# The feed-forward of an encoder layer by Strassen's seven products of 2x2 blocks

## The chip, the cores and the metric

One core of one Trainium2 chip runs the whole program. The metric is the device time of one execution in microseconds (us), the median of several runs. Everything is 32-bit floating point. A matrix product is made of three TensorE passes over operands split in two parts, a rounded high part and the rest: high x high, high x low, low x high (`PASS` in the code).

## The reference

```python
D_MODEL = 1024; SEQ = 1024; DEC_SEQ = 512; DEPTH = 1; D_FF = 2816; NA_HEADS = 16

def rms_norm(x, g):
    y = x * lax.rsqrt(jnp.mean(x * x, axis=-1, keepdims=True) + RMS_EPS)
    return y * g

def swiglu(x, w_gate, w_up, w_down):
    return (jax.nn.silu(x @ w_gate) * (x @ w_up)) @ w_down

def run(x):                                     # DEPTH is 1: one layer
    y = neighbourhood_attention(rms_norm(x, norm_mix[0]), na_w_qkv[0], na_rpb[0], na_w_o[0])
    x = x + y
    x = x + swiglu(rms_norm(x, norm_ffn[0]), ffn_w_gate[0], ffn_w_up[0], ffn_w_down[0])
    return rms_norm(x, norm_final)

return run(x_prompt), run(x_sample)             # (1, 1024, 1024) and (1, 512, 1024)
```

The attention (8 rows x 16 columns of neighbours on a grid, with a bias table) is not touched by the change. The feed-forward is: 1536 tokens by 1024, two products with 1024 x 2816 weights, a gate, and one with 2816 x 1024.

## The kernel before

The 1536 tokens of both requests are one list of `NT` = 12 tiles of 128 tokens. First come the norm, the V projection and the bias tables, then attention by pairs of heads, with the projections of the next pair between its products. The output projection (`project`, L578) of a token tile is work that a list of chores drops in between: TensorE multiplies the attention's output `oh` by `wo`, VectorE adds the residual (L582, tile `xo`), and POOL's DMA queue stores it to `x1_d` in DRAM (L583).

The feed-forward takes the tokens in two chunks of `CH` = 768. `norm2` loads a tile from `x1_d` by ScalarE's DMA queue, `rms` squares it on ScalarE (L107), takes the power -1/2 on POOL (L111) and scales on VectorE (L114); `transpose_split` transposes it on TensorE (L121) and splits it into a high part (ScalarE, L125) and a low one (VectorE, L126). The operands `h2` of a chunk lie in SBUF, transposed, with the model dimension on the partitions.

For each of `NF` = 22 blocks of 128 columns, `gate_up` loads the gate's and the up's weights (`wblock`, SyncE's queue), splits them (`split`: a cast on ScalarE, L130, and a subtraction on VectorE, L131) and makes two halves of 384 tokens, each a group of 24 matmuls of 128x384 (L656). ScalarE's Silu and a product on VectorE (L660, L661) follow, and a split into the operand `gt` of the down projection. After every two blocks (`SL` = 2) `down` multiplies `gt` by the rows of the down weights (L674, 128x512) and adds into `acc` in SBUF (L677), which began as `x1`. `finish` makes the final norm of a tile and stores it. While the first chunk runs, the second chunk's norms are made; its transposes stand before the last `down` of the first chunk.

The order on each engine is that of the code as a scheduler arranges it from the instructions' dependencies; each engine then runs its list strictly in order. Tiles come from pools with a fixed number of buffers, so that an instruction can wait for a buffer's last reader. Pools that are closed give their room to later ones. A DMA waits in its queue's order.

## Time and profile before

| | us |
|---|---|
| median of 3 runs | 1920.95 (1920.31 to 1922.26) |
| profiled execution, span from first to last instruction | 1918.3 |
| TensorE busy in it | 1874.5 (98%) |
| VectorE busy | 957.0 (50%) |
| ScalarE busy | 689.7 (36%) |
| POOL busy | 109.0 (6%) |

The profile is of one execution. In its rows a group of instructions stands with its line, engine, operation, written tile and read tiles, shape and count; then the busy time of all, the mean duration of one in ns, and the idle time of the engine ahead of them with what ended it. Matmuls are pipelined: the busy time divided by the count is the pace, the mean is the latency. A row of the windows table has for a stretch its length, then busy time and count of TensorE, of its weight loads, of VectorE, ScalarE and POOL, then the granted TensorE clock (1.00 is full), the DMA engines' share and GB/s. A row of the timeline has start, length, engine, line and work, and in brackets the idle time before it and what ended it.

### The profile page before, as it was taken

What the parts mean: (1) busy time and instruction counts of PE and PEld (TensorE: products, weight loads), DVE (VectorE), ACT (ScalarE), POOL (GpSimd) and SP (SyncE); (2) the same over time, 40 slices, a digit from 0 to 9 for tenths busy, and PEclk for the clock granted to TensorE, in tenths of its full rate; (3) what the DMA queues carried; (4) which work ended last, traced back from release to release, by engine and by line L of the source; (5) the groups of instructions that cost most, each with busy time, mean ns of one, the idle gap of its engine ahead of it and who ended that gap; (6) DMA issues with size and microseconds to landing.
All of it is one profiled execution on the core that took longest, in us unless ns stands there. A gap on an engine that the chain in (4) does not pass through costs nothing. (4 is left out here: it accounts for less than half of the span.)

```text
span 1918.3 us, 25624 instructions
## 1 busy us (share of the span) xinstructions
PE 1874.5 (98%) x9904; PEld 1641.6 (86%) x9904; DVE 957.0 (50%) x1945; ACT 689.7 (36%) x1414; POOL 109.0 (6%) x184
## 2 busy tenths in 40 slices
PE   8999999999999999999999999999999999999998
PEld 6887777777767778899999999999899999999997
DVE  4402777777885556443344444433634433333434
ACT  4412667666875454322222222221412211121122
POOL 1110000000230001100000000000000000000001
PEclk9999999999999999999999999999999999999999
DMA  7745433333564444652222221212321112222222
GB/s 237 227 163 164 117 102 103 105 104 101 164 186 129 139 132 146 212 194 66 66 66 66 66 66 57 62 59 66 122 66 58 58 61 66 57 66 66 66 66 77
DMA packets 227578, 201.18 MB, mean 105 GB/s; under 512 B 20736, under 2 KB 201216, under 8 KB 227456
## 3 DMA queue, kind: packets, MB, share of 16 engines
q1 hardware_dynamic: 218080, 166.51, 29.5%
q0 software_dynamic: 8512, 29.89, 4.4%
q10 hardware_dynamic: 864, 3.15, 0.5%
q8 instruction: 78, 1.28, 0.3%
q14 instruction: 44, 0.36, 0.1%
HBM read 171.39 MB, written 40.65 MB: 111 GB/s over the span
## 5 line engine op out<-in xcount | busy, mean ns | idle before, releaser
L656 PE MATMUL pgf<-h2b,whl 128*128 128x384 f32 x2112 | 369.0, 334 | 0.0
L656 PE MATMUL pgf<-h,whl 128*128 128x384 f32 x2112 | 368.0, 334 | 0.0
L656 PEld LDWEIGHTS pgf<-h2b,whl 128*128 128x128 f32 x2112 | 366.4, 188 | 1.0
L656 PEld LDWEIGHTS pgf<-h,whl 128*128 128x128 f32 x2112 | 366.4, 188 | 0.8
L674 PE MATMUL pd<-wd,gt 128*128 128x512 f32 x1584 | 365.3, 390 | 0.4 <-DVE acc L677 0.4
L674 PEld LDWEIGHTS pd<-wd,gt 128*128 128x128 f32 x1584 | 296.4, 188 | 60.9 <-DVE acc L677 0.8
L677 DVE TENSOR_TENSOR acc<-acc,pd 128x512 f32<-128x512 f32 x264 | 176.9, 685 | 106.2 <-PE pd L674 106.2
L131 DVE TENSOR_TENSOR whl<-wr,whl 128x1024 fp32r<-128x1024 f32 x104 | 128.5, 1235 | 199.8 <-ACT whl L130 199.8
L660 ACT ACTIVATE sg<-pgf 128x384 f32<-128x384 f32 x88 | 43.3, 491 | 466.9 <-PE pgf L656 466.8
L661 DVE TENSOR_TENSOR sg<-sg,pgf 128x384 f32<-128x384 f32 x88 | 48.8, 554 | 296.7 <-PE pgf L656 296.7
L324 PE MATMUL pg<-hTp,whl 128*128 128x512 f32 x768 | 196.7, 402 | 0.0
L324 PEld LDWEIGHTS pg<-hTp,whl 128*128 128x128 f32 x768 | 139.7, 188 | 29.9 <-issue 0.4
L130 ACT CAST whl<-wr 128x1024 fp32r<-128x1024 f32 x104 | 108.7, 1045 | 120.8 <-issue 110.6
L578 PE MATMUL pgo<-wo,oh 128*128 128x512 f32 x576 | 139.0, 392 | 0.0
L397 ACT ACTIVATE s<-s,mx 128x384 f32<-128x384 f32 (+1 forms) x192 | 110.7, 579 | 67.4 <-DVE mx L394 67.2
L578 PEld LDWEIGHTS pgo<-wo,oh 128*128 128x128 f32 x576 | 105.7, 188 | 20.6
L130 ACT CAST gt<-sg 128x384 fp32r<-128x384 f32 x88 | 44.9, 510 | 185.6 <-DVE sg L661 185.6
L324 PE MATMUL pg<-hTs,whl 128*128 128x512 f32 x384 | 104.0, 407 | 0.8 <-DVE q L335 0.8
L423 PEld LDWEIGHTS po<-pT,v 128*128 128x128 f32 x512 | 74.5, 188 | 31.2 <-DVE pT L416 22.3
L416 DVE TENSOR_TENSOR pT<-ptt,pT 128x384 fp32r<-128x384 f32 (+1 forms) x192 | 89.9, 507 | 20.4 <-ACT pT L415 19.6
L270 PE MATMUL pgv<-wv,hTp 128*128 128x512 f32 x384 | 95.8, 407 | 0.5 <-ACT hTp L125 0.3
L423 PE MATMUL po<-pT,v 128*128 128x256 f32 x512 | 81.8, 288 | 14.6 <-DVE pT L416 14.6
(89 smaller groups left out, 1674.8 us busy)
## 6 DMA issues: line engine op xcount, KB each, us to landing
wr<-ffn_w_gate SPq DMA_DIRECT2D x44, 512.0 KB
wr<-ffn_w_up SPq DMA_DIRECT2D x44, 512.0 KB
wr<-ffn_w_down SPq DMA_DIRECT2D x44, 512.0 KB
wr<-na_w_qkv SPq DMA_DIRECT2D x38, 512.0 KB
vr<-v_d SPq DMA_DIRECT2D x192, 64.0 KB
bp<-in_d SPq DMA_DIRECT2D x48, 192.0 KB
v_d<-vs POOLq DMA_DIRECT2D x24, 256.0 KB, 3.4
es_d<-t_d POOLq DMA_DIRECT2D x8, 768.0 KB, 5.2
```

The source lines that it names most:

```text
L130: nc.scalar.copy(hi, raw)
L131: nc.vector.tensor_tensor(lo, raw, f32(hi), ALU.subtract)
L270: nc.tensor.matmul(pg, hh[a][:, k, c:c + P], wv[k // 2][b][:, k % 2], start=(k == 0 and i == 0), stop=(k == KB - 1 and i == 2))
L324: nc.tensor.matmul(pg, w[:, a, k, :], h[b][:, k, c:c + 512], start=(k == 0 and i == 0), stop=(k == KB - 1 and i == 2))
L397: nc.scalar.activation(s[:, :n], s[:, :n], AF.Exp, bias=mx, scale=-1.0, accum_out=sm)
L416: nc.vector.tensor_tensor(pT[:, :n, 1], pv, f32(pT[:, :n, 0]), ALU.subtract)
L423: nc.tensor.matmul(pos[h][:, g * 256:(g + 1) * 256], vs[c][:, j, h * P:(h + 1) * P], pT[h][:, c].rearrange("p z q -> p (z q)"), start=(c = ...
L578: nc.tensor.matmul(pg, ohs[k // 4][:, a, k % 4], wo[:, b, k, n * 512:(n + 1) * 512], start=(k == 0 and i == 0), stop=(k == KB - 1 and i == 2))
L656: nc.tensor.matmul(pg[:, :384], w[:, a, k], h2[b][:, k, n * 384:(n + 1) * 384], start=(k == 0 and i == 0), stop=(k == KB - 1 and i == 2))
L661: nc.vector.tensor_tensor(sg, sg, pgs[1][:, :384], ALU.mult)
L674: nc.tensor.matmul(pd, gt[:, a, t * P:(t + 1) * P], wd[:, b, n * 512:(n + 1) * 512], start=(f == 0 and i == 0), stop=(f == m - 1 and i == 2))
L677: last = nc.vector.tensor_tensor(av, av, pd, ALU.add)
```

## The change

A product of two matrices that are cut into 2x2 blocks takes eight block products. Strassen's scheme in Winograd's form takes seven, of sums of blocks. With A the weights' blocks (transposed use) and B the tokens' side, the operands are numbered 0 to 6 in the code; the results are sums of the seven.

- The gate and up products are cut in two along the model dimension (512 each), along a pair of column blocks (128 each; `NP` = 11 pairs) and along a chunk's tokens (384 each). `operands` makes the seven token operands: `pair` does it for a tile of the chunk's first half and one of its second. For the first chunk they are split into SBUF (`to_sbuf`), for the second stored to `hop_d` in DRAM (`to_dram`) and loaded between the chunks.
- `w_ops` makes the seven weight operands of a pair with four sums and five splits. `blocks` runs the seven products, each of 12 matmuls of 128x384 (L751), into three PSUM banks: product 0, then 5 and 6 and 3 on top of it, share `pa`; ScalarE (L769, L774, L777) and VectorE (L771, L779, L781) read `pa`, `pb` and `pd` between the products.
- `unit` makes gate and up of a pair, Silu and their product. POOL makes four sums of 384 columns, and seven operands of the down projection go to `gop_d` in DRAM.
- The down projection starts after both chunks. For each of its seven products it splits eleven operands of the down weights (for four of them POOL subtracts two loaded blocks first), loads six tiles of stored activations (`gr`), and runs 33 matmuls of 128x512 (L907) for each; the sums are kept in SBUF (`u2`, `u4`, `c`), and finished token tiles are stored during products 2 and 3.
- `hspool` moves to the left side of SBUF and the raw weights get a pool of their own, since the order in which pools are closed changes.

```diff
-            h2 = [fp.tile([P, KB, CH], F32R, tag=f"h2{z}", name=f"h2{z}") for z in range(2)]
...
+        def operands(dst, xa, xb, tt):
+            b11, b21, b12, b22 = xa[:, :4], xa[:, 4:], xb[:, :4], xb[:, 4:]
+            t1, t2, t3, t4 = (tt[:, n] for n in range(4))
+            dst(0, b11)
+            dst(1, b21)
+            nc.vector.tensor_tensor(t1, b12, b11, ALU.subtract)
+            nc.vector.tensor_tensor(t2, b22, t1, ALU.subtract)
+            dst(5, t2)
+            dst(4, t1)
+            nc.vector.tensor_tensor(t3, b22, b12, ALU.subtract)
+            dst(6, t3)
+            dst(2, b22)
+            nc.vector.tensor_tensor(t4, b21, t2, ALU.subtract)
+            dst(3, t4)
...
+            xn = np_.tile([P, D], F32, tag="xn", name="xn", bufs=3)
+            nc.scalar.dma_start(out=xn, in_=x1_d[t * P:(t + 1) * P, :])
+            xt = np_.tile([P, KB, P], F32, tag="xt", name="xt")
...
+        def to_dram(j):
+            def dst(i, op):
+                nc.sync.dma_start(out=hop_d[i, :, :, j * P:(j + 1) * P], in_=op)
...
+        chores = Chores([oh_job(t) for t in range(TP // P - 1, NT)])
+        for j in range(3):
             chores.do()
             drain(ofill)
-            norm2(0)
-            for t in range(1, CT):
-                norm2(t)
-                chores.do()
-                drain(ofill)
+            pair(0, j, to_sbuf(j))
+        for _ in range(2):
+            chores.do()
+            drain(ofill)
+        for j in range(3):
+            pair(1, j, to_dram(j))
...
-            def gate_up(f, h2):
-                wg = wblock(w_g, f * P)
-                wu = wblock(w_u, f * P)
...
+        def w_ops(w, p):
+            d1 = w_raw(w[:512, p * 256:(p + 1) * 256])
+            d2 = w_raw(w[512:, p * 256:(p + 1) * 256])
+            a11, a21, a12, a22 = d1[:, :, :P], d1[:, :, P:], d2[:, :, :P], d2[:, :, P:]
...
+            ops[0] = one(a11)
+            ops[1] = one(a12)
+            s = sums()
+            nc.vector.tensor_tensor(s[:, 0], a21, a22, ALU.add)
+            nc.vector.tensor_tensor(s[:, 1], s[:, 0], a11, ALU.subtract)
+            ops[4], ops[5] = two(s)
+            r = sums()
+            nc.vector.tensor_tensor(r[:, 0], a11, a21, ALU.subtract)
+            nc.vector.tensor_tensor(r[:, 1], a12, s[:, 1], ALU.subtract)
+            ops[6], ops[2] = two(r)
+            ops[3] = one(a22)
...
+            go(0, pa, True, False)
+            c11 = ctile()
+            nc.scalar.copy(c11, va)
+            go(1, pb, True, True)
+            nc.vector.tensor_tensor(c11, c11, vb, ALU.add)
+            go(5, pa, False, False)
+            c12 = ctile()
+            nc.scalar.copy(c12, va)
+            go(4, pd, True, False)
+            c22 = ctile()
+            nc.scalar.copy(c22, vd)
+            go(6, pa, False, False)
+            nc.vector.tensor_tensor(c22, c22, va, ALU.add)
+            go(2, pd, False, True)
+            nc.vector.tensor_tensor(c12, c12, vd, ALU.add)
+            go(3, pa, False, True)
...
+            nc.gpsimd.tensor_tensor(s[0], a21, a22, ALU.add)
+            nc.gpsimd.tensor_tensor(s[1], s[0], a11, ALU.subtract)
+            nc.gpsimd.tensor_tensor(s[2], a11, a21, ALU.subtract)
+            nc.gpsimd.tensor_tensor(s[3], a12, s[1], ALU.subtract)
+            for i, a in enumerate((a11, a12, s[3], a22, s[0], s[1], s[2])):
+                nc.gpsimd.dma_start(out=gop_d[i, 3 * c:3 * c + 3, :, p].rearrange("j q t -> q j t"),
+                                    in_=a.rearrange("q (j t) -> q j t", j=3))
+        for p in range(NP):
+            unit(0, p, hops)
+        hops2 = [None] * 7
+        for i in (0, 1, 5, 4, 6, 2, 3):
+            o = h_op(i)
+            for k in range(0, KB // 2, 2):
+                r = fr.tile([P, 2, HT], F32, tag="hr", name="hr", bufs=3)
+                nc.sync.dma_start(out=r, in_=hop_d[i, :, k:k + 2])
+                split(r, o[:, 0, k:k + 2], o[:, 1, k:k + 2])
+            hops2[i] = o
+        for p in range(NP):
+            unit(1, p, hops2)
...
-            def down(gw, t, acc):
-                m = len(gw)
-                for n in range(2):
-                    pd = psum("VT"[n], "pd")
-                    for f, (gt, wd) in enumerate(gw):
...
+        for n in (0, 1, 4, 5, 2, 6, 3):
+            wds = [d_op(n, i) for i in range(NP)]
+            for tt in range(6):
+                go = g_op(n, tt)
+                pd = psum("GSVT"[bank % 4], "pd")
+                bank += 1
+                for i in range(NP):
+                    for m, (y, z) in enumerate(PASS):
+                        nc.tensor.matmul(pd, go[:, y, i], wds[i][:, z], start=(i == 0 and m == 0),
+                                         stop=(i == NP - 1 and m == 2))
```

The change writes the feed-forward anew, and with it the order on every engine. Three places show it.

TensorE where the last output projection (`pgo`) ends and the feed-forward begins, before. `pt` is a transpose, `pgf` the gate's product of `h` (two parts) with the first weights `whl`:
```order
L578 MATMUL pgo<-wo,oh 128x512 x48
L121 MATMUL pt<-ident,xn 128x128 x8
L656 MATMUL pgf<-h_8397,whl 128x384
L656 MATMUL pgf<-h_8398,whl 128x384
L656 MATMUL pgf<-h_8397,whl 128x384 x2
```
The same place after; `pa`, `pb`, `pd` are the banks of the products, `wa` and `ws` weight operands, and the numbered `h` the token operands:
```order
L583 MATMUL pgo<-wo,oh 128x512 x94
L665 MATMUL pt<-ident,xn 128x128 x16
L751 MATMUL pa<-h_8407,wa 128x384 x9
L665 MATMUL pt<-ident,xn 128x128 x8
L751 MATMUL pa<-h_8407,wa 128x384 x3
L751 MATMUL pb<-h_8408,wa 128x384 x12
L665 MATMUL pt<-ident,xn 128x128 x8
L751 MATMUL pd<-h_8411,ws 128x384 x12
```
The transposes of the second chunk's tiles moved from the end of the first chunk to this place; two more groups of eight follow some rows later.

ScalarE in the middle of the feed-forward, before (`sg` the Silu, `gt` and `wd` operands of `down`, `whl` weights):
```order
L660 ACTIVATE sg<-pgf 128x384
L130 CAST whl<-wr 128x1024 x2
L130 CAST gt<-sg 128x384
L130 CAST wd<-wr 128x1024
L660 ACTIVATE sg<-pgf 128x384
```
After, an up half and the beginning of the next gate half (`c` are the kept sums, `wt` the weights' sums, `wr` raw weights):
```order
L769 COPY c<-pa 128x384
L135 CAST wa<-wr 128x512 x2
L774 COPY c<-pa 128x384
L777 COPY c<-pd 128x384
L135 CAST ws<-wt 128x1024 x2
L135 CAST wa<-wr 128x512
L769 COPY c<-pa 128x384
L135 CAST wa<-wr 128x512 x2
L789 ACTIVATE c<-c 128x384
```
Copies out of the banks now stand between the casts.

SyncE's DMA queue towards the end, before:
```order
L139 DMA wr<-ffn_w_gate 128x8x128
L139 DMA wr<-ffn_w_up 128x8x128
L139 DMA wr<-ffn_w_down 128x1024
L696 DMA y_prompt<-yo 128x512 x4
L696 DMA y_sample<-yo 128x512 x8
```
After, where the units end and the down projection begins (`dr` raw down weights, `gr` stored activations, `c` a block of `x1`):
```order
L711 DMA wr<-ffn_w_gate 128x4x256 x2
L711 DMA wr<-ffn_w_up 128x4x256 x2
L826 DMA gff<-norm_final 128x1024
L831 DMA dr<-ffn_w_down 128x512 x11
L861 DMA gr<-gop_d 128x1408
L873 DMA c<-x_d 128x512
```
The loads of the down weights moved from each block to the end of the units; the first `dr` shares its place in SBUF with token operand 3, which the last product reads.

301 lines of the change are left out of this document (190 added, 111 removed).

## The prediction, made before the changed kernel was run

> **What bounds the kernel now.** I read the page's busy times first, then the groups of instructions by line, then the windows table for the feed-forward, to see whether TensorE ever waits there.
>
> ```profile
> PE 1874.5 (98%) x9904; PEld 1641.6 (86%) x9904; DVE 957.0 (50%) x1945; ACT 689.7 (36%) x1414; POOL 109.0 (6%) x184
> ```
> ```profile
> L656 PE MATMUL pgf<-h2b,whl 128*128 128x384 f32 x2112 | 369.0, 334 | 0.0
> L656 PE MATMUL pgf<-h,whl 128*128 128x384 f32 x2112 | 368.0, 334 | 0.0
> ...
> L674 PE MATMUL pd<-wd,gt 128*128 128x512 f32 x1584 | 365.3, 390 | 0.4 <-DVE acc L677 0.4
> ...
> L121 PE MATMUL pt<-ident,xn 128*128 128x128 f32 x192 | 27.1, 280 | 7.6 <-DVE xn L114 7.6
> ```
> ```profile
> 860.00:1330.00 470.00, 470.00 (x2512) 444.41 (x2511) 190.11 (x255) 96.53 (x138) 3.30 (x6) 1.00 0.21 63
> 1341.00:1366.00 25.00, 24.65 (x135) 20.14 (x134) 20.60 (x33) 12.62 (x26) 1.47 (x2) 1.00 0.29 96
> 1400.00:1860.00 460.00, 460.00 (x2437) 432.34 (x2436) 183.61 (x247) 89.69 (x127) 0.00 (x0) 1.00 0.22 65
> 1910.00:1918.00 8.00, 0.06 (x1) 0.00 (x0) 4.39 (x8) 1.33 (x4) 1.57 (x2) 0.74 0.53 197
> ```
> ```profile
> 810.73 1.03 PE L121 MATMUL pt<-ident,xn 128*128 128x128 f32 x8
> 811.52 0.77 PE L656 MATMUL pgf<-h,whl 128*128 128x384 f32 x3
> ```
> ```profile
> 1905.82 4.24 PE L674 MATMUL pd<-wd,gt 128*128 128x512 f32 x18
> ```
>
> The feed-forward runs from 811.52 to 1905.82 + 4.24 = 1910.06 us, and in it TensorE is busy 470 of 470 and 460 of 460 us (second column of the windows rows) at clock 1.00; at the change of chunk it is idle for 0.35 of 25 us. VectorE is busy for 40% of it, ScalarE for 20%, POOL hardly. So only TensorE's work counts, and 1098.5 us of the 1918.3 us span are this stage. The 369.0 + 368.0 us over 4224 matmuls make 174.5 ns each (the mean of 334 ns is a latency; they overlap), the down projection 365.3 / 1584 = 230.6 ns each.
>
> **Matmuls.** Gate and up drop from 4224 to 3696 of the same 128x384 shape, down from 1584 to 1386 of the same 128x512 shape: both are 7/8. The 48 transposes of the second chunk move ahead of the stage, and at 27.1 us for 192 they are 6.8 us either way. So 1098.5 - 6.8 = 1091.7 us become 955.2: **-136.5 us**, if every operand is there in time.
>
> **VectorE, ScalarE and POOL in a unit** (a pair of gate column blocks and a pair of up blocks, 168 matmuls, 168 x 174.5 ns = 29.3 us).
>
> ```profile
> L661 DVE TENSOR_TENSOR sg<-sg,pgf 128x384 f32<-128x384 f32 x88 | 48.8, 554 | 296.7 <-PE pgf L656 296.7
> L131 DVE TENSOR_TENSOR whl<-wr,whl 128x1024 fp32r<-128x1024 f32 x104 | 128.5, 1235 | 199.8 <-ACT whl L130 199.8
> L131 DVE TENSOR_TENSOR oh<-wr,oh 128x512 fp32r<-128x512 f32 x24 | 16.4, 685 | 5.4 <-ACT oh L130 5.3
> L130 ACT CAST whl<-wr 128x1024 fp32r<-128x1024 f32 x104 | 108.7, 1045 | 120.8 <-issue 110.6 <-PE pgf L656 5.5 <-DMA wr<-ffn_w_up 3.2
> L130 ACT CAST oh<-wr 128x512 fp32r<-128x512 f32 x24 | 14.8, 619 | 29.0 <-PE pgo L578 21.8 <-DMA wr<-o_d 6.2 <-PE pss L386 0.7
> L660 ACT ACTIVATE sg<-pgf 128x384 f32<-128x384 f32 x88 | 43.3, 491 | 466.9 <-PE pgf L656 466.8
> ```
>
> VectorE per half unit: three splits and four sums of 512 columns (7 x 0.685), two splits of 1024 (2 x 1.235), three adds of 384 (3 x 0.554), 8.9 us; twice, with four products at 0.554, 20.1 us of 29.3. ScalarE: per half unit three casts (0.619), two (1.045), three copies of 384 out of PSUM (0.491, by the Silu row): 5.4 us; twice, with four Silu, 12.8 us. Neither becomes the bound by its sum. What matters is the order in their queues, because the first, third, fifth and seventh product accumulate into one bank, `pa`, and ScalarE or VectorE must read it in between. The order leaves one other product, 12 x 174.5 ns = 2.09 us, for each read. The copies (L774, L777) take 0.49 and stand behind nothing that waits for a later product. The tightest is the add L779, due 2.09 us after the fifth product: ahead of it stands the split of a `ws`, whose cast follows the copy L777. Counted from the end of the fourth product: copy 0.49, cast 1.05, split 1.24, add 0.55 end at 3.3 us, due at 4.2. Slack 0.9 us less semaphores, so I take **0 us of waiting** in the 44 half units. Without that cover each lost microsecond costs 44 us. Weights are split half a unit ahead, so they don't press.
>
> POOL is new here: four sums of 384 columns and seven stores. That is where engines can collide:
>
> ```profile
> 524.72 8.95 POOL L507 TENSOR_TENSOR wo<-or,wo 128x1024 fp32r<-128x1024 f32 x3 [8.94 <-ACT wo L506]
> 533.60 0.55 POOL L453 DMA_DIRECT2D o_d<-oT  x1
> 534.17 2.39 POOL L507 TENSOR_TENSOR wo<-or,wo 128x1024 fp32r<-128x1024 f32 x1
> ```
> ```profile
> 526.80 2.22 DVE L131 TENSOR_TENSOR whl<-wr,whl 128x1024 fp32r<-128x1024 f32 x1
> ...
> 534.02 2.70 DVE L401 TENSOR_SCALAR s<-s,ri 128x256 f32<-128x256 f32 x1
> ```
>
> A split that lasts 1.235 us on the mean lasts 2.22 beside a POOL sum, and the normalization at 534.02 ends with POOL's at about 536.6: VectorE stood still while POOL ran. At 2.39 us for 1024 columns a sum of 384 takes 0.90 us; POOL has 4 x 0.90 + 7 x 0.55 = 7.5 us per unit, and can hold VectorE up by 3.6 us, 23.7 of 29.3 in all. The sums come at the end of a unit, five products before the next L779, so I let them cost nothing; had every hold-up reached TensorE, the sum would be 22 x 3.6 = 79 us worse, which is a rival below. The Trainium skill, SBUF — State Buffer, section "Who interferes with whom", states this as a rule: a VectorE instruction with two SBUF inputs and a GpSimd one that reads SBUF shut each other out for the whole instruction. These rows agree with it: 2.22 against 1.235 us.
>
> A unit also stores seven blocks of 197 KB and loads four of 524 KB, 3.5 MB in 29.3 us or 119 GB/s, where the windows above have 63 to 65 and earlier slices (below) over 200: hidden.
>
> **From the norms to the units (A).** Before, the second chunk's norms and transposes lay among the down products; now all stand ahead of the first units, and their operands go to DRAM.
>
> On TensorE the transposes of these six tiles, 48 by the order, now stand between the first products of the first two half units (the rows shown with the change).
>
> ```profile
> x_d<-xo POOLq DMA_DIRECT2D x24, 256.0 KB, 3.6
> ```
> ```profile
> 766.02 0.33 ACTq L624 DMA_DIRECT2D xn<-x_d  x1
> 770.01 1.06 ACT L107 ACTIVATE junk<-xn 128x1024 f32<-128x1024 f32 x1 [3.48 <-DMA xn<-x_d]
> 770.98 0.18 ACT L107 ACTIVATION_READ_ACCUMULATOR junk<-xn 128x1 f32 x1
> 772.49 1.06 ACT L107 ACTIVATE junk<-xn 128x1024 f32<-128x1024 f32 x1 [1.33 <-DMA xn<-x_d]
> ```
> ```profile
> L114 DVE SCALAR_TENSOR_TENSOR xn<-xn,rs,gbf 128x1024 f32<-128x1024 f32 x6 | 7.7, 1285 | 5.7 <-POOL rs L111 5.7
> L111 POOL TENSOR_TENSOR rs<-me,mhalf 128x1 f32<-128x1 f32 x24 | 13.4, 557 | 456.7 <-DVE me L109 456.7
> L125 ACT CAST h<-pt 128x512 fp32r<-128x512 f32 x12 | 6.5, 585 | 10.9 <-PE pt L121 10.9
> ```
>
> The weight operands lie where the output projection's tiles lay, so the first cast waits for the last `xo` store: add 0.7, issue 0.55, landing 3.6, 4.9 us after the last projection. The second chunk's tiles go through two `xt` buffers, in three rounds: a round's Square waits until the round before has landed in DRAM (3.6 us by the store row; queueing takes it towards 5), then 1.24 Square, 0.56 power, 1.29 scale, about 1 transposes, 1.2 copies. Two such rounds of 9 to 10 us, some 3 us before them and 3 for the second tile of the last one make 24 to 30 us until ScalarE's queue reaches the copy of the first product, without which the third cannot start; the rounds share VectorE with the first weights, so I take 30. TensorE has until then 72 product matmuls (12.6 us) and 48 transposes (6.8): 10.6 us idle. After it the queues, now behind, cost some 6 us more (adds and casts in one row). The 21 stores of these operands (262 KB each) stand in SyncE's queue between the first weight loads; that is in the rounds' 5 us. **+17**, bounds 8 (all but the first 5 and 3 us overlapped) and 24 (the 30 us with no transposes as cover: 30 - 12.6 + 6). The first chunk's norms, in pairs among output projections: VectorE has per pair two scales (2.6), four sums (2.7) and seven splits (4.8), with evictions some 12.6 us, against 48 projections and 16 transposes: **+1.5**, 0 to 3. The reload of the seven operands between the chunks (14 loads of 384 KB through three buffers; each next operand is due a full half unit, 14.7 us, after its last use): **+2**, 0 to 5.
>
> **From the units to the down projection (C).** The down weights came with each block; now eleven loads, then the activations, stand at the end, and the first waits, since `dr` lies where the last product's operand lay.
>
> ```profile
> GB/s 237 227 163 164 117 102 103 105 104 101 164 186 129 139 132 146 212 194 66 66 66 66 66 66 57 62 59 66 122 66 58 58 61 66 57 66 66 66 66 77
> ```
> ```profile
> 785.97 0.38 SPq L139 DMA_DIRECT2D wr<-ffn_w_gate  x1
> ```
> ```profile
> 790.15 1.05 ACT L130 CAST whl<-wr 128x1024 fp32r<-128x1024 f32 x1 [1.24 <-DMA wr<-ffn_w_gate]
> ```
> ```profile
> 20.00:24.00 4.00, 4.00 (x21) 3.14 (x22) 2.48 (x4) 1.87 (x4) 0.33 (x1) 1.00 1.13 336
> ```
> A load's first use comes 4.2 us after its issue. 11 x 262 KB + 721 KB = 3.6 MB at the 336 GB/s of this window take 10.7 us; with 3 to 4 us of latency and a cast of 1408 columns (1.375 x 1.045 = 1.4) TensorE starts about **16 us** after the last product. Bounds 12 (latency inside) and 22 (the 237 GB/s of the page's first slice).
>
> **Down stage.** Per row of 33 matmuls 7.6 us; the next activations need 1.4 + 1.65 on two engines. Weights are split into 17 buffers while the last row runs, one each 0.69 us, as fast as VectorE's 0.685. Loads of a product: 11 or 22 x 262 KB and 6 x 721 KB, 7.2 or 10.1 MB in 45.7 us, 158 or 221 GB/s. Whole slices of 48 us ran at 237, so it fits, barely: **+4**, 0 to 15.
>
> **Cold starts.**
> ```profile
> 7.55 1.94 PE L121 MATMUL pt<-ident,xn 128*128 128x128 f32 x8 [7.55 <-DVE xn L114]
> 9.64 9.04 PE L270 MATMUL pgv<-wv,hTp 128*128 128x512 f32 x24
> 18.51 1.04 PE L121 MATMUL pt<-ident,xn 128*128 128x128 f32 x8
> ...
> 21.65 7.95 PE L270 MATMUL pgv<-wv,hTp 128*128 128x512 f32 x33
> ```
> After 7.55 us of idleness eight transposes took 1.94 us, later 1.04; 24 matmuls took 9.04 where 33 took 7.95 (24 would be 5.8). A restart costs 0.9 to 4.1 us; two: **+2**, 2 to 8. By the Trainium skill, TensorE: Matmul & The Clock Gate, "What's actually happening", the clock halves after some 3.4 us of idleness and stays so for as long: 1.7 us each, 3.4 in the sum; the transposes agree.
>
> **Sum.** 1918.3 - 136.5 + 17 + 1.5 + 2 + 16 + 4 + 2 = 1824.3 us of span; the median of the runs (1920.95) stands 2.65 above the profiled span, the tail after the last matmul stays as it is: **1827 us**, own range 1808 to 1850. All low ends give 1807, all high ends 1861. Below 0.2% (4 us) this kernel's runs cannot tell a difference.
>
> **Rivals.**
> - *A short wait in each half unit*: the 0.9 us of slack is eaten by semaphores and by queues that slip. Against: nothing in the rows waits so now; for: the same bank was never read between matmuls. 1 us each: 1871.
> - *POOL holds VectorE up and all of it reaches TensorE*: 1827 + 79 = 1906. Against: the sums lie five products from the tight add.
> - *The down stage is bound by loads*: at 163 GB/s (the page's third slice) the two products of 10.1 MB take 62 us instead of 45.7, +32: 1859.
> - *The transitions hide*: 1807, if A and C take their low ends.
> - *Shorter matmul groups (12, not 24) pace worse*: 3% of 645 us, 1846; no row shows it.
> - *Slower than before*: a read of `pa` stands in ScalarE's queue behind a cast that waits for the next product to end. Then each half unit loses 2.09 + 0.49 = 2.6 us: 1827 + 44 x 2.6 = 1941. It decides from 2.1 us per half unit (94 us). Against: every cast ahead of a read waits only for products already run.
> - That it saves no matmuls is excluded by the order.
>
> **Chances.** Forecast 0.58, short waits 0.14, loads 0.07, hidden 0.07, POOL 0.06, pace 0.04, slower 0.04. Only the last is slower: faster 0.95, same 0.01, slower 0.04. 1806 to 1880 leaves out part of the short waits, POOL and the slow case, about 2 in 10.
>
> **What the profile after would show.** Right: L751 near 174 ns and L907 near 231 ns each with idle times near 0 in the windows of the units; two gaps, about 17 us spread over the first two units, ending with the copy L769, and about 16 us before L907, ending with `dr` and `gr`. Wrong: idle time of L751 laid to L774, L777 or L779 (short waits); VectorE's splits and sums longer than 0.7 and 1.24 (POOL); L907 waiting for `go` in every row (loads).

## The result and the profile after

The kernel after takes 1861.22 us (median; 1858.81 to 1861.7) against 1921.61 us for the kernel before in the same comparison: 0.968 of the time (95% interval 0.967 to 0.969), 60 us less. Forecast were 1827 us, 94 less. The profiled execution spans 1859.4 us where the sum of the prediction gave 1824.3, so 35.1 us are to be explained. First the page's busy times of the kernel after.

```profile
PE 1764.7 (95%) x9178; PEld 1520.4 (82%) x9178; DVE 1192.7 (64%) x2191; ACT 864.8 (47%) x1706; POOL 447.3 (24%) x494
```

TensorE has the 726 matmuls less that were forecast, but it is no longer busy throughout: 95% instead of 98%. What it waits for is told by the table of its waits, by line with total, number and longest wait in us. These are the rows of the feed-forward; those of the attention are left out:

```profile
PE pd L907 <- ACT go L135: 19.3, 2, 16.6
PE pd L907 <- DVE go L136: 10.5, 8, 4.1
PE pa L751 <- ACT wa L135: 5.1, 2, 4.9
PE pt L665 <- DVE xn L119: 3.7, 3, 3.0
PE pb L751 <- DVE c L771: 3.6, 1, 3.6
PE pa L751 <- ACT c L774: 2.0, 1, 2.0
PE pa L751 <- DVE wa L136: 1.2, 1, 1.2
PE pd L751 <- ACT h L135: 0.9, 1, 0.9
PE pa L751 <- ACT c L769: 0.8, 1, 0.8
PE pa L751 <- ACT h L135: 0.6, 1, 0.6
PE pd L751 <- DVE h L136: 0.6, 1, 0.6
PE pa L751 <- DVE h L136: 0.5, 1, 0.5
PE pt L665 <- ACT xt L666: 0.3, 1, 0.3
```

The single 16.6 is the gap before the down projection (C). The rest of the first two rows, 13.2 us, lies inside the down projection. The rows that wait for `h`, and the one that waits for `c L774`, are the reload between the chunks (B): 4.6 us. The others are the start of the units (A): 14.7 us.

In the steady part of the units the timeline shows nothing but matmuls. These two rows are the same place in two units that follow each other:

```profile
883.33 4.32 PE L751 MATMUL pa<-h,wa 128*128 128x384 f32 x24
...
912.56 4.32 PE L751 MATMUL pa<-h,wa 128*128 128x384 f32 x24
```

168 matmuls in 29.23 us, 174.0 ns each, and no wait in the rows. The kernel before, start to start, for its two shapes:

```profile
1463.38 33.44 PE L656 MATMUL pgf<-h2b,whl 128*128 128x384 f32 x192
1496.66 16.49 PE L674 MATMUL pd<-wd,gt 128*128 128x512 f32 x72
1512.99 33.44 PE L656 MATMUL pgf<-h2b,whl 128*128 128x384 f32 x192
```

That is 33.28 us / 192 = 173.3 ns for 384 columns and 16.33 / 72 = 226.8 ns for 512. The down projection after does not keep the second pace. Timeline of the kernel after, one TensorE row ahead of the gap's end and some of those inside the down projection; then a row of the windows table (length, busy time and count of TensorE, its weight loads, VectorE, ScalarE, POOL, then the granted clock, DMA share, GB/s):

```profile
1507.07 1.22 PE L907 MATMUL pd<-wd,go 128*128 128x512 f32 x2 [16.64 <-ACT go L135]
...
1712.75 15.67 PE L907 MATMUL pd<-wd,go 128*128 128x512 f32 x66 [1.91 <-DVE go L136]
...
1737.84 7.96 PE L907 MATMUL pd<-wd,go 128*128 128x512 f32 x33 [1.28 <-DVE go L136]
...
1772.89 78.34 PE L907 MATMUL pd<-wd,go 128*128 128x512 f32 x328 [4.06 <-DVE go L136]
```
```profile
1768.00:1788.00 20.00, 15.94 (x62) 12.46 (x61) 10.48 (x11) 2.74 (x2) 7.10 (x4) 0.91 0.47 159
```

From 1507.07 to 1772.89 + 78.34 = 1851.23 us the down projection takes 344.2 us; forecast were 319.3. The waits stand ahead of rows of 33 matmuls in the fifth and sixth of the seven products (numbers 2 and 6, from about 1710 us on), and after the longer ones the clock falls for a while.

The start of the units, with the timeline and two windows:

```profile
819.36 3.33 PE L751 MATMUL pa<-h,wa 128*128 128x384 f32 x9 [4.91 <-ACT wa L135]
825.72 1.94 PE L665 MATMUL pt<-ident,xn 128*128 128x128 f32 x8 [3.03 <-DVE xn L119]
```
```profile
819.30:826.00 6.70, 3.61 (x11) 2.91 (x12) 3.76 (x6) 2.53 (x6) 0.87 (x1) 0.50 1.12 354
...
856.00:862.00 6.00, 6.00 (x28) 6.00 (x28) 2.89 (x6) 1.66 (x3) 0.00 (x0) 0.76 0.67 250
```

The last projection ends at 812.1 us, and until 862 TensorE alternates between waits and matmuls. By further windows the clock is 0.50 to 0.53 from 819 to 832 us, 1.00 from 832 to 850, and 0.68 and 0.76 from 850 to 862. By stages, in us (measured pieces that no row gives directly are the stage's length less the others):

| piece | forecast | measured |
|---|---|---|
| output projections before A | +1.5 | +0.6 |
| 3696 matmuls of 384 columns | 640.5 | 643.1 |
| A: waits and slow clock | 17 + 1 | 23.8 |
| B: reload of the operands | 2 | 4.6 |
| C: gap before the down projection | 16 | 16.6 |
| 1386 matmuls of 512 columns | 314.3 | 323.5 |
| down projection: waits and slow clock | 4 + 1 | 20.7 |

The differences add up to 35.6 us; the span missed by 35.1. Nearly half of it, 15.7, is the waits inside the down projection with the slow clock after them, and a quarter, 9.2, is a slower pace there. The experiments take these two first, then the transitions. Where a run's time is compared with the kernel after, that one counts as 0.968 of the kernel before on the same chip, 1858 to 1859 us. One execution of one run below took 2147 us at a mean granted clock of 0.75 and is left out of that run's time.

### The profile page after: what moved, and what is told of

Read it like the earlier page. It is cut to its first block, busy times and chain, and to the rows that moved or that the text cites. A ratio compares the mean times of both kernels' runs of the same rounds, so it can differ in the third digit from the quotient of the medians.

```text
span 1859.4 us, 25647 instructions
## 1 busy us (share of the span) xinstructions
PE 1764.7 (95%) x9178; PEld 1520.4 (82%) x9178; DVE 1192.7 (64%) x2191; ACT 864.8 (47%) x1706; POOL 447.3 (24%) x494
## 4 chain that ended last, share of the span: by engine, by line
PE 67%; DVE 11%; DMA 10%; ACT 6%; issue 3%; SPq 2%; POOL 2%; DVEq 0%; POOLq 0%; ACTq 0%
PE pa L751 19%; PE pd L907 13%; PE pd L751 9%; PE pgv L275 7%; DMA vr<-v_d 5%; PE pg L329 5%; PE pb L751 5%; PE pgo L583 4%; DVE pT L421 2%; SPq L375 2%; DMA dr<-ffn_w_down 1%; ACT s L402 1%; PE pss L391 1%; PE ptt L417 1%; PE po L428 1%
## 5 line engine op out<-in xcount | busy, mean ns | idle before, releaser
L907 PE MATMUL pd<-wd,go 128*128 128x512 f32 x1386 | 331.0, 400 | 29.8 <-ACT go L135 19.3
L907 PEld LDWEIGHTS pd<-wd,go 128*128 128x128 f32 x1386 | 262.4, 190 | 98.3 <-ACT go L135 20.3
L751 PE MATMUL pa<-h,ws 128*128 128x384 f32 x1056 | 201.5, 340 | 2.8 <-ACT c L774 2.0
L751 PE MATMUL pa<-h,wa 128*128 128x384 f32 x1056 | 194.1, 339 | 7.4 <-ACT wa L135 5.1
L751 PE MATMUL pd<-h,ws 128*128 128x384 f32 x1056 | 198.6, 337 | 1.5 <-ACT h L135 0.9
L751 PEld LDWEIGHTS pa<-h,wa 128*128 128x128 f32 x1056 | 184.9, 190 | 9.2 <-ACT wa L135 5.6
L751 PEld LDWEIGHTS pa<-h,ws 128*128 128x128 f32 x1056 | 184.6, 190 | 6.7 <-ACT c L774 5.3
L136 DVE TENSOR_TENSOR ws<-wt,ws 128x1024 fp32r<-128x1024 f32 x88 | 108.5, 1234 | 126.5 <-ACT ws L135 126.3
L751 PEld LDWEIGHTS pd<-h,ws 128*128 128x128 f32 x1056 | 184.7, 188 | 2.1 <-ACT h L135 1.2
L329 PEld LDWEIGHTS pg<-hTp,whl 128*128 128x128 f32 x768 | 140.2, 189 | 29.8 <-issue 0.4
L136 DVE TENSOR_TENSOR wa<-wr,wa 128x512 fp32r<-128x512 f32 x132 | 117.9, 897 | 18.8 <-ACT wa L135 18.2
L751 PE MATMUL pb<-h,wa 128*128 128x384 f32 x528 | 101.8, 342 | 3.6 <-DVE c L771 3.6
```

What stands on the lines that cost most here:

```text
L136: nc.vector.tensor_tensor(lo, raw, f32(hi), ALU.subtract)
L329: nc.tensor.matmul(pg, w[:, a, k, :], h[b][:, k, c:c + 512], start=(k == 0 and i == 0), stop=(k == KB - 1 and i == 2))
L751: nc.tensor.matmul(bank[:, :HT], a(y, k), b[:, z, k], start=start and k == 0 and i == 0, stop=k == KB // 2 - 1 and i == 2, skip_group_chec ...
L907: nc.tensor.matmul(pd, go[:, y, i], wds[i][:, z], start=(i == 0 and m == 0), stop=(i == NP - 1 and m == 2))
```

## Experiments: the waits inside the down projection

The weights of products 6 and 3 are differences that POOL makes while the product ahead, 2 or 6, runs; in the same time the tiles that product 2 finishes are normalized and stored. Timeline of the kernel after, all engines but TensorE, 10 us of product 2:

```profile
1735.01 1.00 SPq L890 DMA_DIRECT2D y_prompt<-yo  x2
...
1736.12 0.90 SPq L831 DMA_DIRECT2D dr<-ffn_w_down  x2
...
1741.75 1.29 POOL L854 TENSOR_TENSOR dr<-dr 128x512 f32<-128x512 f32 x1 [7.32 <-DMA dr<-ffn_w_down]
1743.00 0.55 POOL L886 TENSOR_TENSOR rs<-me,mhalf 128x1 f32<-128x1 f32 x1
1743.58 1.41 DVE L889 SCALAR_TENSOR_TENSOR yo<-c,rs,gff 128x512 f32<-128x512 f32 x2 [5.67 <-POOL rs L886]
...
1745.51 1.62 DVE L136 TENSOR_TENSOR go<-gr,go 128x1408 fp32r<-128x1408 f32 x1
```

Read from the bottom: the split of `go`, for which TensorE waits, stands on VectorE behind the scaling L889; that one waited 5.67 us for the power L886, which stands on POOL behind a subtraction L854 that waited 7.32 us for a load; and the load stands on SyncE behind the stores L890 of the tile that was scaled before. Read so, it is a ring through the lists of POOL and VectorE and SyncE's queue, each worked off in its order. Two runs move one link each.

**The subtractions on VectorE.**

```diff
-                nc.gpsimd.tensor_tensor(b, d_raw(i, 1, 0), b, ALU.subtract)
+                nc.vector.tensor_tensor(b, d_raw(i, 1, 0), b, ALU.subtract)
...
-                nc.gpsimd.tensor_tensor(b, b, d_raw(i, 0, 1), ALU.subtract)
+                nc.vector.tensor_tensor(b, b, d_raw(i, 0, 1), ALU.subtract)
```

> The subtractions of down weights for products 6 and 3 (22 of 44) go from POOL to VectorE; nothing else changes. Theory of the ring: in product 2 and at the start of product 6 the final norm's power on POOL stands behind a subtraction that waits for a load, the load stands in SyncE's queue behind a store that waits for that norm, and TensorE waits for the split behind it on VectorE. Without POOL in the ring the 12.3 us of idle time between 1710 and 1773 us fall to 0 to 4, with some 4 us of cold clock: about 1847 (1843 to 1851). Rival one: the loads' rate binds there (216 to 259 GB/s in those slices); then the idle time stays and the time is 1859 to 1863. Rival two: VectorE, with 22 x 0.69 = 15 us more, becomes what TensorE waits for: 1862 to 1875.

Measured: 1841.36 us, ratio 0.960 (0.958 to 0.961), 17 us less than the kernel after. The last 955 of the 1386 matmuls are one row of the timeline:

```profile
1607.97 223.09 PE L907 MATMUL pd<-wd,go 128*128 128x512 f32 x955 [0.49 <-DVE go L136]
```

POOL's subtractions are the cause: with them on VectorE, and the same loads and stores in the same queues, TensorE waits less than 1 us in the whole down projection, which then takes 327.4 us instead of 344.2. So 16.8 of the 20.7 us came from this link (the waits and the slow clock after them). The time is 2 us under the theory's range. Both rivals are out: the loads are as many as before, and VectorE has more to do.

**The stores on ScalarE's queue.**

```diff
-                nc.sync.dma_start(out=yrow(t)[:, hs], in_=y)
+                nc.scalar.dma_start(out=yrow(t)[:, hs], in_=y)
```

> The 24 stores of the result go from SyncE's queue to ScalarE's; nothing else changes. The ring theory: the loads of down weights no longer stand behind stores that wait for the norm, so POOL's subtractions get their data and the norm's power comes in time: the idle time between 1710 and 1773 us falls from 12.3 to 0 to 5 us, time about 1848 (1844 to 1853). Rival: the stores now hold up ScalarE's casts, which stand behind them in its order, as long as the norm takes (about 4 us per tile): idle time of the same size or more, laid to the casts of go, 1858 to 1875. Under a bound by transfer rate nothing changes: 1859 to 1863.

Measured: 1864.76 us, ratio 0.972 (0.971 to 0.974): no gain, some 7 us slower than the kernel after. The rival came true. The stores now stand on ScalarE ahead of the casts of `go`, and the cast waits for the scaling that the store waits for:

```profile
1731.73 1.38 ACT L135 CAST go<-gr 128x1408 fp32r<-128x1408 f32 x1 [4.84 <-DVE yo L889]
```

TensorE is idle for 13.3 us inside the down projection, as before (13.1). One hold-up took the place of another, so this run says nothing about the link through the stores. That POOL's subtractions cause the waits is shown; that the ring closes through the stores is read from the rows and not shown by a run.

## Experiments: the pace of the 512-column matmuls

233 ns instead of 227 is 9 us of 1386 matmuls. The waits don't explain it, since it stands in rows without any. It can be read from VectorE, which takes each result as soon as it is done; here two of six such adds that follow each other, in the kernel after:

```profile
1617.90 0.69 DVE L916 TENSOR_TENSOR u<-u,pd 128x512 f32<-128x512 f32 x1 [4.25 <-PE pd L907]
1625.61 0.69 DVE L916 TENSOR_TENSOR u<-u,pd 128x512 f32<-128x512 f32 x1 [4.67 <-PE pd L907]
```

7.71 us for 33 matmuls, 233.6 ns. One thing that differs between L907 and L674 is where in a block of 512 bytes the two operands' tiles begin in a partition of SBUF: in L674 both at 480, in L907 `wd` at 480 and `go` at 32.

```diff
+        dl.tile([P, 112], F32, name="pad")
         gf = dl.tile([P, D], F32, name="gff")
```

> A pad of 448 bytes is put at the bottom of the pool that holds the activation tiles of the down stage, so that the tiles go begin at byte 93152 and 104416 of each partition instead of 92704 and 103968 (480 instead of 32 over a multiple of 512); the tiles wd stay where they are, and no instruction is added, removed or moved. What is disputed is why the 512-column matmuls of L907 take 233.4 ns each where those of L674 took 226.8. Theory (alignment): the pace follows from where the two operands begin in a block of 512 bytes: in both kernels 512-column matmuls whose two operands begin alike (480 and 480, or 32 and 32) go at 227 ns and those that begin differently at 233 ns. Then a row of 33 takes 7.49 us instead of 7.70 and the down stage is 1386 x 6.6 ns = 9 us shorter: about 1849 us against 1858. Rival (something else of the stage, such as the longer run of 33 into one bank, the separate tiles of wd or the other traffic): rows stay at 7.70 us and the time at 1858.

Measured: 1851.65 us, ratio 0.965 (0.963 to 0.966), about 7 us less than the kernel after. The same adds:

```profile
1618.84 0.69 DVE L917 TENSOR_TENSOR u<-u,pd 128x512 f32<-128x512 f32 x1 [4.44 <-PE pd L908]
1626.32 0.69 DVE L917 TENSOR_TENSOR u<-u,pd 128x512 f32<-128x512 f32 x1 [4.44 <-PE pd L908]
```

7.48 us for 33, 226.7 ns, the pace of the kernel before, with the same instructions in the same order: the place of the tiles is the cause. (The pad moves all tiles of that pool by 448 bytes; of the two operands of these matmuls only `go` is among them.) Of the 9 us only 7 show in the time, because the waits are still there: waits and slow clock take 23.5 us of the down projection's 337.7, where they took 20.7 of 344.2. The last run below moves the tiles of another line and finds the same.

## Experiments: the gap before the down projection (C)

**The loads' places.** The prediction had the loads wait for `dr`'s place. Here the tiles `tk`, `u2` and `u4` are taken when they are first used, so that `dr` and `gr` lie where the operands of earlier products lay.

```diff
-        keep = [dl.tile([P, 512], F32, tag="tk", name="tk", bufs=NP) for _ in range(NP)]
+        keep = []
...
+                keep.append(dl.tile([P, 512], F32, tag="tk", name="tk", bufs=NP))
                 b = keep[i]
                 nc.gpsimd.tensor_tensor(b, d_raw(i, 0, 1), d_raw(i, 0, 0), ALU.subtract)
```

> Same work; only the places in SBUF change: the raw down weights (dr) and the stored activations (gr) now lie where token operands 0, 1 and 2 lay, which the last units are done with earlier than with operand 3. Theory: the 16.64 us in which TensorE idles between the units and the down projection are the loads' own time, made to start late by the shared place; then the first loads start some 12 us earlier, the gap falls to 2 to 7 us, and the time to about 1849 (1846 to 1852), a restart of the clock (about 2 us) included where the gap stays under 3 us. Rival: the gap is bound by transfer rate, casts and splits (11 casts and splits of about 0.7 us each and 3.6 MB), which cannot begin earlier; then the gap stays at 14 to 16 us and the time at 1859 to 1861.

Measured: 1857.69 us, ratio 0.968 (0.967 to 0.970): no gain. The gap became 15.82 us, and the timeline shows why:

```profile
1488.77 7.55 DVE L136 TENSOR_TENSOR wd<-dr,wd 128x512 fp32r<-128x512 f32 x8
...
1495.13 0.33 SPq L862 DMA_DIRECT2D gr<-gop_d  x1
...
1504.07 1.22 PE L907 MATMUL pd<-wd,go 128*128 128x512 f32 x2 [15.82 <-ACT go L135]
```

Six loads come early now (the first is issued at 1475.80 us, 1490.46 in the kernel after), but their splits stand on VectorE behind the last unit's products, the other five need a buffer that these splits free, and the first activations are issued on SyncE behind them all, at 1495.13 us. The place was one wait of several that end at nearly the same time; alone it does not set the gap.

**The first activations loaded second.** With the early places, and with the subtractions on VectorE:

```diff
-            wds = [d_op(n, i) for i in range(NP)]
+            if n == 0:
+                wds = [d_op(0, 0)]
+                first = g_op(0, 0)
+                wds += [d_op(0, i) for i in range(1, NP)]
+            else:
+                wds = [d_op(n, i) for i in range(NP)]
...
-                go = g_op(n, tt)
+                go = first if (n, tt) == (0, 0) else g_op(n, tt)
```

> Three edits together: the subtractions for products 6 and 3 on VectorE, the early places of dr and gr, and the first stored activations (gr) loaded second in SyncE's queue instead of twelfth. The same work is done. Theory: between the units and the down projection the loads of dr 7 to 11 wait for splits of the first six, which stand on VectorE behind the unit's last product, and gr stands behind them in the queue; with gr ahead, TensorE can begin when the first split is made, 3 to 5 us after the last product, and then waits operand by operand some 3 to 6 us in the first row: the gap of 17.1 us falls to 5 to 10 us in all, the time from 1841 to 1831 (1828 to 1835). Rival: the 11 loads' transfer and splits bind it whatever the order; then the first row takes 14 to 16 us instead and the time stays at 1839 to 1842.

Measured: 1833.65 us, ratio 0.956 (0.954 to 0.957), 8 us less than with the subtractions alone. The first row of 33 now runs piece by piece as its operands come, in part at a slow clock (0.50 from 1494 to 1497 us):

```profile
1488.10 0.39 PE L912 MATMUL pd<-wd,go 128*128 128x512 f32 x1
...
1493.94 9.70 PE L912 MATMUL pd<-wd,go 128*128 128x512 f32 x29 [0.18 <-DVE wd L136]
1505.23 0.92 PE L912 MATMUL pd<-wd,go 128*128 128x512 f32 x2 [1.59 <-ACT go L135]
```

So the gap was set by the order of the loads in one queue together with the place; the place alone gave nothing, and the order alone was not tried.

## Experiments: the start of the units (A)

**Another order of the tiles**, so that each pair's two tiles are ready early and the pairs of both chunks alternate:

```diff
-        chores = Chores([oh_job(t) for t in range(TP // P - 1, NT)])
-        for j in range(3):
-            chores.do()
-            drain(ofill)
-            pair(0, j, to_sbuf(j))
-        for _ in range(2):
-            chores.do()
-            drain(ofill)
-        for j in range(3):
-            pair(1, j, to_dram(j))
+        chores = Chores([oh_job(t) for t in (9, 7, 10, 8, 11)])
+        for todo in (((1, 0),), ((0, 0),), ((1, 1),), ((0, 1),), ((0, 2), (1, 2))):
+            chores.do()
+            drain(ofill)
+            for c, j in todo:
+                pair(c, j, to_dram(j) if c else to_sbuf(j))
```

> The last five token tiles are projected in the order 9, 7, 10, 8, 11 instead of 7 to 11, and the pairs of the second chunk stand among those of the first, so that only two pairs are left after the last projection instead of three; the work is the same. Theory: the start of the units costs 24 us (14.7 us idle and about 9 us at a cold clock) since three rounds of square, scale, transpose and store follow each other there; with one pair of the second chunk left after the last projection the start costs 8 to 14 us, and the time is about 1848 (1845 to 1853). Rival: the start is bound by the weights' own loads, casts and splits behind the output projection's tiles, which stay: 1857 to 1862. Rival two: VectorE, with some 58 us of pairs against 55 us of projections, holds up the projections: 1855 to 1866.

Measured: 1871.09 us, ratio 0.975 (0.974 to 0.977), 13 us slower. Two rows of TensorE's table of waits:

```profile
PE pt L665 <- DVE xn L119: 13.1, 9, 5.6
...
PE pt L665 <- DVE me L114: 8.6, 2, 7.9
```

The transposes now stand in TensorE's list ahead of projections that could run, and wait for tiles that are stored and loaded again; the two longest waits, 5.6 and 7.9 us, still come after the last projection. The order of the kernel after covers the chain behind each tile better than this one.

**The second chunk's sums left out**, so its operands are plain blocks and VectorE has 12 sums less; the kernel leaves out that part of the computation.

```diff
+            if c:
+                for i, b in enumerate((b11, b21, b22, b12, b11, b21, b12)):
+                    dst(i, b)
+                return
```

> The sums of the second chunk's token operands are left out: seven plain blocks are stored instead of three blocks and four sums, so VectorE has 12 sums of 512 columns (8.2 us) less before and among the first units, with as many stores; the second chunk's output is not the reference's. Theory now: the start of the units is bound by VectorE's work there (5 to 6 busy of each 6 us between 826 and 850 us), so the start is 6 to 9 us shorter: 1852 to 1855. Rival, the prediction's: rounds of square, scale, transpose and store through two xt buffers bind it; all seven stores read xt now, so the rounds are as long or longer: 1860 to 1866.

Measured: 1857.54 us, ratio 0.968 (0.967 to 0.969): no gain, between the forecasts of theory and rival. Less work on VectorE did not shorten A. The run does not take VectorE's work away alone, though: all seven stores now read `xt`, and the next Square waits until they have landed (to 821.35 us, 821.04 in the kernel after, although the last projection ended 1.3 us earlier).

**TensorE kept warm** by transposes that nobody reads, 45 in A's first gap and 150 in C's:

```diff
+        def idle(after, n):
+            with tc.issue_after(after.ins):
+                pt = psum("T", "pt")
+                for _ in range(n):
+                    nc.tensor.transpose(pt[:, :P], ident, ident)
```

> TensorE makes 45 transposes of a constant (about 4.5 us) in the idle time after the last norms' transposes and 150 (about 15 us) in the gap before the down projection; nobody reads them, all else is the same. Theory: the granted clock of 0.50 to 0.53 from 819 to 832 us and of 0.51 at 1507 to 1511 us is the price of the idle time, some 5 us at the first place and 2 at the second; kept busy, TensorE runs at full clock there: 1853 to 1856. Rival: the product matmuls there wait for operands anyway and the low clock hides under those waits, or the transposes come late themselves: 1859 to 1864.

Measured: 1859.19 us, ratio 0.969 (0.967 to 0.970): no gain, neither from A nor from C. A's first gap, a window, and the wait that follows:

```profile
812.00:819.00 7.00, 5.82 (x50) 5.34 (x48) 3.28 (x5) 1.75 (x4) 0.00 (x0) 1.00 1.02 318
```
```profile
824.28 1.94 PE L671 MATMUL pt<-ident,xn 128*128 128x128 f32 x8 [6.21 <-DVE xn L119]
```

The clock is 1.00 up to product 0, whose first matmuls ran at 0.50 in the kernel after, and the wait for the next normalized tile grows from 3.03 to 6.21 us. In A the slow clock had only filled time in which TensorE would have waited. In C the clock of the first rows rose too (0.85 from 1506 to 1510 us, against 0.51 from 1507 to 1511), but the gap took 17.2 us instead of 16.6 and the down projection 343.2 instead of 344.2. The Trainium skill, TensorE: Matmul & The Clock Gate, "What's actually happening", has the clock halve after an idle window; the 0.50 after 4.91 us and the 1.00 with the dummy work agree.

**The first weights earlier.** The first cast's tile no longer lies over a tile `xo` whose store must land, and the second load goes to a buffer that is free earlier.

```diff
-            r = rpool.tile([P, 1024], F32, tag="raw", name="wr") if turn[0] % 5 < 2 else \
+            r = rpool.tile([P, 1024], F32, tag="raw", name="wr") if turn[0] % 5 in (1, 2) else \
...
+        fr.tile([P, 2, KB // 2, P], F32R, tag="wa", name="wa", bufs=6)
         for p in range(NP):
             unit(0, p, hops)
```

> The first cast of weights of the gate and up stage is given a place that does not lie over the tiles xo of the last projections (one buffer of wa is skipped), and the second load of weights goes to a buffer that is free earlier, so it is issued ahead of the stores of the last norms. Nothing is left out. Theory (what sets the start of the stage is the landing of the last results' store at about 818.7 us, since the first cast lies over xo, and the second load, 7.8 us behind the stores): product 0 starts at about 814.5 us instead of 819.4, some 20 instead of 9 matmuls stand ahead of the transposes of the next pair, and the stage gains 3 to 6 us: about 1853 to 1855 us against 1858. Rival (the waits only move, as in the two runs that shortened work at this place: the transposes wait for the normalized tile, whose square waits until the stores of xt have landed): product 0 starts earlier, the wait before the transposes grows from 3.0 to 6 us or more, and the time stays within 2 us of 1858.

Measured: 1856.37 us, ratio 0.968 (0.966 to 0.969): within what the runs can tell from no change, on the side of a gain of 2 us. The first wait fell from 4.91 us to two short ones, and the next ones stand:

```profile
817.17 3.57 PE L751 MATMUL pa<-h,wa 128*128 128x384 f32 x10 [1.19 <-DVE wa L136]
...
828.54 1.94 PE L665 MATMUL pt<-ident,xn 128*128 128x128 f32 x8 [2.94 <-DVE xn L119]
```

Between the gain and "the waits only move" this run does not decide: the time lies just above the theory's range and at the edge of the rival's, but the wait that should have grown by the rival did not. The runs together say that fewer sums on VectorE, a full clock and earlier first weights, each by itself, gain little or nothing in A. What is left is the chain store, reload, square, power, scale, transposes of each round, as the prediction laid it out; that it alone sets A was not shown by a run that shortens it.

## Experiments: POOL and VectorE in the units

```diff
-            nc.gpsimd.tensor_tensor(s[0], a21, a22, ALU.add)
+            nc.vector.tensor_tensor(s[0], a21, a22, ALU.add)
```

and so for the unit's other three sums.

> The four sums of a unit go from POOL to VectorE. Theory: in the units POOL's sums hold VectorE up (the mean split of 512 columns is 897 ns instead of 685), but this reaches TensorE nowhere: the mean falls to 690 to 720 ns, VectorE gets 4 x 0.55 us per unit more, and the time stays at 1859 to 1862 with the pace of 29.23 us per unit. Rival: the hold-ups do cost TensorE small waits that the profile hides in the matmuls' modelled ends; then 1850 to 1857.

Measured: 1853.64 us, ratio 0.966 (0.965 to 0.968), some 4 us less, at the edge of what can be told. Splits of `wa`, first in the kernel after, then here:

```profile
L136 DVE TENSOR_TENSOR wa<-wr,wa 128x512 fp32r<-128x512 f32 x132 | 117.9, 897 | 18.8 <-ACT wa L135 18.2
```
```profile
L136 DVE TENSOR_TENSOR wa<-wr,wa 128x512 fp32r<-128x512 f32 x132 | 90.1, 687 | 19.7 <-ACT wa L135 18.0
```

The hold-up is as large as thought, 28 us of VectorE's time for this group alone, and little of it reached TensorE, but not nothing: the rival holds. In this run the rows of 24 matmuls that lie a unit apart begin at 876.97 and 906.09 us, so a unit takes 29.12 us instead of 29.23 and a matmul 173.3 ns, as in the kernel before. In the kernel after every second half unit takes 14.67 us instead of 14.56, which the rows do not show as a wait; that is 2.4 us if all 22 units are alike. The waits of the reload (B) are 2.0 us instead of 4.6. That a VectorE instruction with two inputs in SBUF and a POOL instruction that reads SBUF shut each other out is the rule of the Trainium skill's SBUF — State Buffer, "Who interferes with whom"; 897 against 687 ns agrees.

## Experiments: all parts together

The parts that gained, and the first weights, in one kernel:

> The parts that gained or might gain are put together: the subtractions of products 3 and 6 and the sums of the gate and up units on VectorE, the places of the down stage's tiles taken when they are needed, the first tile of activations loaded second, the go tiles 448 bytes further up, and the first weights of the gate and up stage in places that are free earlier. Nothing is left out. Theory (the costs are separate): 1834 us of the version with the first activation tile early, less 3 to 4 us for the sums, less 9 us for the pace of 1386 matmuls (all of it, since without the ring at products 3 and 6 nothing else limits those rows), less about 2 us for the first weights: about 1819 to 1822 us, rows of 7.48 us through the whole down stage. Rival (the faster rows run into the next limit, the loads of dr and gr on SyncE's queue or VectorE's added work): waits of TensorE on go or wd appear in the middle of the down stage and the time stays at 1825 us or more.

Measured: 1813.71 us, ratio 0.944 (0.943 to 0.946), 45 us less than the kernel after and 107 less than the kernel before. The page's group of the down projection shows that most of the waits are gone (7.4 us of idle time, where the two rows of waits on `go` above make 29.8):

```profile
L914 PE MATMUL pd<-wd,go 128*128 128x512 f32 x1386 | 319.8, 392 | 7.4 <-DVE go L136 3.0
```

The costs were separate, as the theory had it; the time is even 5 us below its lower end. By the traces the stage from the last projection to the last unit is 7.3 us shorter than in the run with the first activations early, and the down projection 10.1, where the theory had 5 to 6 and 9; the rest of the 5 us was not settled. In the last kernel the pad lies at the bottom of SBUF instead, and moves all tiles of the left side:

```diff
+        cpool.tile([P, 112], F32, name="pad")
         mhalf = cpool.tile([P, 1], F32, name="mhalf")
```

> As the run with all parts together, but the pad of 448 bytes lies at the very bottom, so that all tiles of the left side move up by it: the weight tiles whl of the attention's projections and the activations hTs begin at 480 over a multiple of 512 (32 before), like hTp, go, wd, wo and oh; the operands h of the gate and up products go from 32 to 480 too, and the value weights wv from 416 to 352, still unlike their partner at 480. Theory (alignment of the two operands within 512 bytes): the 512-column matmuls of L329 on hTp go from 233.4 to 227 ns each (768 of them, 5 us at most, less where the attention stage waits for other engines), those on hTs stay at 227, those of the value projection stay at 233, and the time is 2 to 5 us under that of the run with all parts. Rival (the place matters in another way, for instance only the stationary operand's or only in the down stage): L329 stays at 233.4 ns, or the value projection changes too, and the time is the same as with all parts.

Measured: 1811.83 us, ratio 0.943 (0.942 to 0.945). The attention's first run of projections, before (with all parts) and now:

```profile
157.19 23.03 PE L329 MATMUL pg<-hTp,whl 128*128 128x512 f32 x98
```
```profile
156.79 22.42 PE L330 MATMUL pg<-hTp,whl 128*128 128x512 f32 x98
```

235 and 229 ns each, by the same shift in another stage: the theory of the place holds for a second line. The value projection, whose operands still begin unlike (352 and 480), stayed: 7.94 us for 33 matmuls, 7.95 in the kernel before.

```profile
20.84 7.94 PE L276 MATMUL pgv<-wv,hTp 128*128 128x512 f32 x33
```

The 2 us of time are at the theory's lower end and not to be told from none. This is the fastest version tried.

## Why the prediction was right, and where it missed

- **The bound and the sign** were right: only TensorE's work counted before, an eighth of it went, and the units run nearly without a wait in all but a few of the 44 half units. The rival of a short wait in each half unit is out as priced (1 us each; the runs show 0.11 us in every second one), and so is the one of an add or copy behind a waiting cast.
- **Matmuls, -136.5**: measured -124.6 (gate and up 732.0 to 643.1, down 359.2 to 323.5). The step that failed is that the same shape keeps its pace. For 512 columns 233.4 against 226.8 ns cost 9.2 us, by the place of `go` in SBUF. For 384 columns 174.0 against 173.3 cost 2.6 us, but that is POOL's hold-up and not pace: with POOL's sums on VectorE it is 173.3. The rival "shorter groups pace worse" named the wrong line: the groups of 12 do not, the rows of 33 do for another reason. (The prediction's 174.5 and 230.6 ns divide busy times in which neighbouring rows overlap; start to start they are 173.3 and 226.8. Its sum goes by the span and is not touched by this.)
- **Down stage, +4 (0 to 15)**: mis-sized, 19.7 without the cold start counted apart. I weighed it by the bytes of the loads against the DMA's rate and by VectorE's work; neither was the limit. POOL's subtractions, behind which the norm's power and so VectorE's list stood, were in no step, although the sums on POOL and the stores of finished tiles in the same products stood in the change. With them on VectorE 327.4 - 323.5 = 3.9 us are left, with the cold start in them, about what was forecast. The rival "bound by loads" priced products 4 and 6; the waits stand in 2 and 6, where the weights of 6 and 3 are made, and they went with the same loads, so its cause is wrong.
- **C, +16 (12 to 22)**: the size was right (16.64), the reason half of it. Taking the place's wait away gave nothing; place and order in the queue together gave 8 us.
- **A, +17 (8 to 24)**: waits of 14.7 us, and 9 us of matmuls at a lower clock, together the upper end. I had the cold starts as a term of their own, +2 for two; the runs show that they lie within the waits, so that the chain's length, not their sum, is the price.
- **B, +2 (0 to 5)**: 4.6, mis-sized within its bounds.
- **POOL's hold-up at nothing**: too low by some 4 us, of a possible 79; 2.4 of them are the 0.11 us in each unit.
- The own range, 1808 to 1850, missed by 11 us; POOL's subtractions in the down projection (16.8) and the place of `go` (9.2) alone are more. The time lies within 1806 to 1880, whose upper part had been left to rivals that did not come true as priced, and that it equals what all high ends of the sum give, 1861, is luck: C and the projections stayed far below their high ends, the down stage went beyond its own, and the 11.9 us of the matmuls had no bounds.

## What to carry to other kernels

When work is spread over engines that each run a list in order, look for chains that may close to a ring: an instruction that waits for a load, ahead of one that a store waits for, ahead of the next load in the same queue. Bytes and busy times do not show them. Which link to move has to be tried: here the subtractions moved to VectorE removed the waits, and the stores moved to ScalarE's queue put others in their place. A price for one shape may hold only for the line it was measured on, so compare the pace of several lines of the same shape, and where they differ, compare where their operands lie. A slow clock or a wait that is followed by another wait may cost nothing by itself, as at the start of the units here; then take it away together with the next one.

## What the runs showed of the hardware that was not expected

The pace of fp32r matmuls of 512 columns depends on where the two operands begin within 512 bytes of a partition: 233.6 ns with 480 and 32, 226.7 ns with 480 and 480, with the same matmuls in the same order (7.71 against 7.48 us for 33). For 384 columns no difference was seen: in the last run, with both of L751's operands at 480, a unit takes 29.12 us, 173.3 ns per matmul, which L656 had in the kernel before:

```profile
876.31 4.32 PE L752 MATMUL pa<-h,wa 128*128 128x384 f32 x24
...
905.43 4.32 PE L752 MATMUL pa<-h,wa 128*128 128x384 f32 x24
```

The kernel with all parts, and the one with only POOL's sums on VectorE, have the same 29.12 us with L751's operands still at 32 and 480. Which of the lower bits of the address decide was not tried; the two lines were only moved by 448 bytes.
